# Where a depthwise convolution's taps run: from VectorE, ScalarE and GpSimd to diagonal products on TensorE, inside a mixed decoder block

## The chip, the cores and the metric

One core of a Trainium2 chip runs the whole block for 1024 tokens. The metric is the device time of one execution in microseconds; lower is better. The kernel before takes 3563.5 us (median of three runs, 3561.2 to 3568.37).

## What is computed

One decoder block over x (1024 tokens, 1024 channels), in float32:

```python
u = modulate(rmsnorm(x, norm_mix_g), sh_mix, sc_mix)
p = u @ w_in
y_conv = conformer_conv(p[..., :1024], ...)   # GLU, causal depthwise conv of 31 taps, LayerNorm, SiLU; 512 channels
y_rwkv = rwkv7_mix(p[..., 1024:], ...)        # linear recurrence over tokens, 8 heads of 64
x = x + gt_mix * (concat([y_conv, y_rwkv]) @ w_out)
u = modulate(rmsnorm(x, norm_ffn_g), sh_ffn, sc_ffn)
x = x + gt_ffn * peer_ffn(u, ...)             # product keys choose 8 x 16 of 16384 experts per token
return rmsnorm(x, final_g)
```

The change concerns one line of it, the depthwise convolution: each of 512 channels is filtered with its own 31 weights, `y[t, ch] = sum_j w[j, ch] * in[t - 30 + j, ch] + b[ch]`. Channels lie on partitions, so that 512 channels are four blocks of 128 partitions, and a tap is a multiply-add with one scalar per partition over the tokens of a step.

## The kernel before

All work is written as Python generators ("streams") that yield one instruction at a time. At build time a planner (`Issue.go`, L250) always takes the stream whose next instruction could start first by its own table of durations, and hands the instruction to a scheduler that orders each engine's queue by priority among what is ready. `AHEAD` (L77) moves instructions of some streams forward by a number of places: the recurrence (b), the expert choice (d) and the taps by 300, fetching and using expert rows by 1000; others not at all. At run time each engine works its queue strictly in that order.

The program has two stages.

First stage. Tokens go in five steps (`MACROS`, L65: 128, 128, 256, 256, 256 tokens, that is tiles 0; 1; 2 and 3; 4 and 5; 6 and 7 of 128 tokens).
- Stream a (L549 to L612) multiplies u by w_in (PSUM tile `pA`): first the 14 blocks for the recurrence, written to `xs`, then the 8 blocks of the convolution, whose gated result is `yin` (one buffer, with 30 tokens of the step before in front). It begins `yin` of a step only when the convolution of the step before is over (L602).
- The taps streams (L655 to L689) filter `yin` into `cb`, one 128-channel block after the other. `CONV` (L74) names for each of the four blocks the way it takes: v is VectorE, one multiply-add per tap; g is ScalarE and GpSimd, where ScalarE scales a shifted `yin` into `tap` and GpSimd adds it to `cb`; p is TensorE, below.
- Stream l (L615 to L651) normalises `cb` over channels through PSUM tile `pL` (one buffer) and writes the first half of `ym`.
- Stream b (L698 to L949) runs the recurrence tile by tile, strictly one after the other since each needs the state of the last; many small dependent products (PSUM `pB`) with VectorE and ScalarE steps between them. It writes the second half of `ym` (`ym<-y`).
- Stream c (L952 to L1038) multiplies `ym` by w_out (`pC<-ym,wtC`) when both halves of a step are there, then forms the expert queries (`pC<-uC,wtC`, `pC<-kt,qT`); stream d (L1041) chooses the experts on VectorE and GpSimd.
- For tiles 0, 3, 6 and 7 (`GATHER`) the chosen experts' rows are fetched by GpSimd DMAs (`row`) and used on VectorE (`row<-row,u`, `acc<-row,hj,acc`), in both stages. For tiles 1, 2, 4 and 5 streams g and h turn the choice into a gate matrix through one-hot products (`pA<-onea,oneb`), written to DRAM.

Second stage. Once the first-stage streams a, b, l, y, g, h and the taps are over and all w_out products are done (L1382), tiles 1, 2, 4 and 5 are run through all 16384 experts on TensorE (`ph`, `po`, `pC<-ch`), while the remaining rows are used beside it.

The way p, there already for a block marked p: for each tap ScalarE writes a diagonal matrix, `ident` scaled by the tap's weight (`dg`, 128x128, L660), in pairs that alternate between the buffers of `sqL` and `rsL`; TensorE adds `dg` times the shifted `yin` into one `pL` tile (L663), and after 31 taps ScalarE moves the sum to `cb` with the bias (L664).

Of the kernel before, what the change touches and what calls it, by code (L numbers as in the profile page):

```python
# [70 lines left out]
BIAS = {('use', 'DVE'): 0.0, ('useg', 'POOL'): 0.0, ('a', 'PE'): 0.0}  # L71
DoneDict = dict
ORDER = 'blcdaghy'
ROWS, PSA, CONV = 3, 2, 'vvgg'  # L74
HG = (2, 8)

AHEAD = {('fetch', None): 1000, ('use', None): 1000, ('useg', None): 1000, ('b', None): 300, ('d', None): 300, ('taps', None): 300}  # L77
# [1526 lines left out]
```

## Time and profile before

| | us |
|---|---|
| three runs | 3561.2, 3563.5, 3568.37 |
| profiled execution | 3577.81 |
| its span, first to last instruction | 3576.1 |
| TensorE busy (matmul) | 3119.0 (87%) |
| VectorE busy | 2709.2 (76%) |
| GpSimd busy | 2107.5 (59%) |
| ScalarE busy | 1571.2 (44%) |

In the views PE is TensorE's matmuls, PEld its weight loads, DVE is VectorE, ACT ScalarE, POOL GpSimd. A float32 product is recorded as two MATMUL passes. Nearly every instruction goes through one helper, so that lines say little (L220) and tile names, written out<-in, tell the work. Matmul ends are modelled, so that a busy PE need not be a PE at its peak; PEclk is the granted TensorE clock as a share of 2.4 GHz.

### The profile page before, as it was taken

The page shows a single profiled execution, that of the slowest core. Times are in us where ns is not written, and L with a number is a line of the kernel's source. Part 1 is how long each engine was busy: PE and PEld are TensorE (multiplying, and loading weights), DVE is VectorE, ACT ScalarE, POOL GpSimd, SP SyncE. Part 2 cuts the span into 40 slices and gives each one's busy share as a digit, 9 for nine tenths or more (in the row PEclk, how much of TensorE's full clock was granted, in tenths as well). Part 3 has the DMA queues.
Part 4 walks back from the last instruction along what each step waited for, and adds up shares of the span by engine and source line. Part 5 has one row for each costly group of instructions (what it writes and reads, how often), then busy time and mean ns, then how long its engine had stood idle before and what let it go on. Part 6 is the DMA issues. An engine that isn't in the chain of part 4 may idle for free. (4 is left out here: it accounts for less than half of the span.)

```text
span 3576.1 us, 54020 instructions
## 1 busy us (share of the span) xinstructions
PE 3119.0 (87%) x18460; PEld 2553.7 (71%) x18460; DVE 2709.2 (76%) x5824; ACT 1571.2 (44%) x3831; POOL 2107.5 (59%) x2024
## 2 busy tenths in 40 slices
PE   4999998896899989786783799999999999999996
PEld 4788776775787767665672577777777777777784
DVE  5755888899868878888899977676666777776664
ACT  3445636537554534643764333333333333333332
POOL 0304647579754745667776866565655665665561
PEclk9798988896899988877896899999999999999998
DMA  6654776774677436656787699898988989999982
GB/s 200 218 184 153 282 261 216 272 273 176 213 267 271 145 107 221 239 202 212 277 311 267 220 327 327 314 319 297 324 310 311 331 312 312 336 324 315 324 275 83
DMA packets 423938, 923.02 MB, mean 258 GB/s; under 512 B 30448, under 2 KB 263024, under 8 KB 354032
## 3 DMA queue, kind: packets, MB, share of 16 engines
q0 software_dynamic: 73728, 536.90, 41.0%
q1 hardware_dynamic: 349936, 382.67, 33.2%
q8 instruction: 147, 2.41, 0.3%
q14 instruction: 127, 1.04, 0.1%
HBM read 873.33 MB, written 46.14 MB: 257 GB/s over the span
## 5 line engine op out<-in xcount | busy, mean ns | idle before, releaser
L220 POOL DMA_INDIRECT row<-in_peer_uv_dram,idx x512 | 542.9, 1060 | 464.8 <-DVE ap L220 165.2
L220 POOL TENSOR_TENSOR vl<-v,vh 128x512 fp32r<-128x512 f32 x256 | 329.3, 1292 | 217.3 <-ACT vh L220 211.9
L220 POOL TENSOR_TENSOR wl<-w,wh 128x1024 fp32r<-128x1024 f32 x128 | 307.7, 2404 | 184.2 <-ACT wh L220 183.9
L220 DVE SCALAR_TENSOR_TENSOR ap<-row,hj,ap 128x1024 f32<-128x1024 f32 x280 | 360.0, 1286 | 65.4 <-ACT hj L220 64.2
L220 DVE CUSTOM_DVE_ANT_0 row<-row,up 128x1024 f32<-128x1024 f32 x283 | 344.1, 1216 | 66.3 <-DMA row<-in_peer_uv_dram,idx 65.4
L220 PE MATMUL pA<-uA,wtA 128*128 128x256 f32 (+1 forms) x1760 | 359.8, 358 | 8.8 <-ACT xs L220 5.0
L220 DVE SCALAR_TENSOR_TENSOR acc<-row,hj,acc 128x1024 f32<-128x1024 f32 x224 | 324.0, 1446 | 44.2 <-ACT hj L220 43.3
L220 POOL TENSOR_TENSOR cb<-cb,tap 128x256 f32<-128x256 f32 (+1 forms) x300 | 244.9, 817 | 153.3 <-ACT tap L220 137.0
L220 PEld LDWEIGHTS pA<-uA,wtA 128*128 128x128 f32 x1760 | 297.6, 203 | 48.0 <-ACT xs L220 5.5
L220 PE MATMUL ph<-uh,wh 128*128 128x512 f32 x1024 | 273.2, 412 | 57.1 <-ACT wh L220 50.1
L220 ACT ACTIVATE hj<-hj 128x1 f32<-128x1 f32 x512 | 101.4, 200 | 449.8 <-DVE hj L220 448.8
L220 ACT CAST vh<-v 128x512 fp32r<-128x512 f32 x256 | 155.2, 617 | 308.4 <-DMA v<-in_peer_uv_dram 181.5
L220 PE MATMUL pC<-uC,wtC 128*128 128x256 f32 (+1 forms) x1280 | 276.4, 372 | 16.0 <-ACT s L220 8.9
L220 DVE CUSTOM_DVE_ANT_0 row<-row,u 128x1024 f32<-128x1024 f32 x171 | 242.6, 1421 | 49.0 <-DMA row<-in_peer_uv_dram,idx 48.9
L220 PEld LDWEIGHTS ph<-uh,wh 128*128 128x128 f32 x1024 | 202.8, 200 | 105.6 <-ACT wh L220 50.4
L220 PE MATMUL po<-ch,vh 128*128 128x512 f32 x512 | 210.4, 411 | 66.0 <-ACT ch L220 39.2
L220 PEld LDWEIGHTS pC<-uC,wtC 128*128 128x128 f32 x1280 | 228.1, 213 | 50.1 <-ACT s L220 10.8
L220 PE MATMUL ph<-ul,wh 128*128 128x512 f32 x1024 | 258.2, 389 | 0.0
L220 PE MATMUL ph<-uh,wl 128*128 128x512 f32 x1024 | 257.6, 394 | 0.0
L220 ACT CAST wh<-w 128x1024 fp32r<-128x1024 f32 x128 | 134.1, 1049 | 217.5 <-PE ph L220 131.1
L220 PEld LDWEIGHTS ph<-uh,wl 128*128 128x128 f32 x1024 | 196.6, 192 | 42.2
L220 DVE TENSOR_TENSOR ph<-ph,gt 128x256 f32<-128x256 f32 x256 | 110.0, 430 | 147.9 <-ACT ph L220 146.0
(323 smaller groups left out, 7548.9 us busy)
## 6 DMA issues: line engine op xcount, KB each, us to landing
v<-in_peer_uv_dram SPq DMA_DIRECT2D x256, 256.0 KB, 6.2
w<-in_peer_uT_dram SPq DMA_DIRECT2D x128, 512.0 KB, 5.4
wtA<-in_w_in_dram SPq DMA_DIRECT2D x220, 256.0 KB, 3.9
wtC<-in_w_q_dram SPq DMA_DIRECT2D x160, 256.0 KB, 4.7
Gd<-stg SPq DMA_DIRECT2D x32, 1024.0 KB, 5.7
gt<-Gd SPq DMA_DIRECT2D x31, 1024.0 KB, 13.4
wtC<-in_w_out_dram SPq DMA_DIRECT2D x80, 256.0 KB, 3.2
wtC<-in_ada_w_dram SPq DMA_DIRECT2D x64, 256.0 KB, 3.9
```

The source lines that it names most:

```text
L220: r = op.fn(*op.a, **op.k)
```

## The change

One letter string: every one of the four channel blocks takes the way p.

```diff
-ROWS, PSA, CONV = 3, 2, 'vvgg'
+ROWS, PSA, CONV = 3, 2, 'pppp'
```

`stream_taps` is made once for each letter in `CONV` (L1373), so that two streams (g and v) become one, which does the four blocks one after the other; `taps_dve` and `taps_pool` are no longer called. The function that is now called for all four:

```python
def taps_pe(yin, o, c, n):
    ps = pL()[:, :n]
    for j in range(TAPS):
        if j % 2 == 0:
            dg = tl(act, [128, 2, 128], "dg", tag=("sqL", "rsL")[j // 2 % 2])
        yield A.activation(dg[:, j % 2, :], ident, AF.Copy, scale=cv("dw_w", c * TAPS + j, 1))
        if j % 2 or j == TAPS - 1:
            for q in range(j - j % 2, j + 1):
                yield PE.matmul(ps, dg[:, q % 2, :], yin[:, c, q:q + n], start=q == 0, stop=q == TAPS - 1)
    yield A.activation(o, ps, AF.Identity, bias=cv("dw_b", c, 1))
```

## Rows read from the trace of the kernel before

**Rows 1.** Page parts 1 and 2: busy us and share; PE in 40 slices.

```profile
PE 3119.0 (87%) x18460; PEld 2553.7 (71%) x18460; DVE 2709.2 (76%) x5824; ACT 1571.2 (44%) x3831; POOL 2107.5 (59%) x2024
PE   4999998896899989786783799999999999999996
```

**Rows 2.** Busy time in four stretches: stretch, length, busy us by engine, PEclk, DMA.

```profile
0.00:100.00 100.00, 53.99 (x364) 49.53 (x365) 52.92 (x153) 34.97 (x105) 9.94 (x29) 1.00 0.67 213
100.00:1290.00 1190.00, 1083.42 (x8328) 893.51 (x8328) 943.76 (x2231) 625.53 (x1657) 693.87 (x779) 0.87 0.64 220
1290.00:1968.00 678.00, 505.38 (x3541) 422.25 (x3539) 585.30 (x1807) 353.28 (x816) 451.33 (x489) 0.81 0.68 238
1968.00:3576.00 1608.00, 1476.17 (x6232) 1188.45 (x6232) 1127.25 (x1636) 557.41 (x1255) 952.34 (x728) 0.96 0.86 298
```

**Rows 3.** Timeline of DVE: ends of recurrence tiles 0, 5, 7 (start, us).

```profile
229.81 1.12 DVE L220 SCALAR_TENSOR_TENSOR ym<-y,col,pB 128x128 f32<-128x128 f32 x4
...
1271.62 1.11 DVE L220 SCALAR_TENSOR_TENSOR ym<-y,col,pB 128x128 f32<-128x128 f32 x4
...
1659.12 0.33 DVE L220 SCALAR_TENSOR_TENSOR ym<-y,col,pB 128x128 f32<-128x128 f32 x1
```

**Rows 4.** Timeline of PE: queries, w_out, one-hot products, second stage's start.

```profile
1256.38 0.71 PE L220 MATMUL pC<-kt,qT 128*128 128x128 f32 x4
...
1257.56 2.61 PE L220 MATMUL pC<-ym,wtC 128*128 128x128 f32 x21
...
1703.36 0.61 PE L220 MATMUL pA<-onea,oneb 128*128 128x128 f32 x4
...
1917.63 0.77 PE L220 MATMUL pA<-onea,oneb 128*128 128x128 f32 x2 [2.27 <-DVE onea L220]
1968.46 2.07 PE L220 MATMUL ph<-uh,wh 128*128 128x512 f32 x4 [50.06 <-ACT wh L220]
```

**Rows 5.** Busy time in the stretches of recurrence tiles 3, 5 and 6.

```profile
633.00:872.00 239.00, 201.97 (x1423) 163.09 (x1422) 215.15 (x467) 129.12 (x351) 176.41 (x174) 0.84 0.71 248
...
1080.00:1273.00 193.00, 176.17 (x1289) 141.12 (x1288) 166.81 (x473) 90.77 (x232) 108.18 (x113) 0.89 0.55 193
1273.00:1466.00 193.00, 175.65 (x1367) 142.02 (x1366) 152.92 (x477) 83.25 (x202) 108.85 (x123) 0.86 0.53 185
```

**Rows 6.** Groups by shape: taps on three engines (busy us, mean ns, idle before).

```profile
L220 POOL TENSOR_TENSOR cb<-cb,tap 128x256 f32<-128x256 f32 x180 | 179.0, 995 | 43.5 <-ACT tap L220 35.5 <-ACT hj L220 0.4
...
L220 DVE SCALAR_TENSOR_TENSOR cb<-yin,col,cb 128x256 f32<-128x256 f32 x180 | 124.8, 712 | 0.6
...
L220 ACT ACTIVATE tap<-yin,col 128x256 f32<-128x256 f32 x180 | 89.6, 505 | 72.0 <-POOL cb L220 71.3
...
L220 POOL TENSOR_TENSOR cb<-cb,tap 128x128 f32<-128x128 f32 x120 | 65.9, 549 | 109.8 <-ACT tap L220 101.4 <-ACT pb L220 2.3
...
L220 ACT ACTIVATE tap<-yin,col 128x128 f32<-128x128 f32 x120 | 46.1, 398 | 16.5 <-POOL cb L220 12.5
...
L220 DVE SCALAR_TENSOR_TENSOR cb<-yin,col,cb 128x128 f32<-128x128 f32 x120 | 45.0, 400 | 1.4
```

**Rows 7.** Groups by shape: products and a scaling like those that are added.

```profile
L220 PE MATMUL pA<-uA,wtA 128*128 128x256 f32 x1056 | 262.7, 402 | 5.0 <-ACT xs L220 4.3 <-DVE yin L220 0.5
...
L220 PE MATMUL pA<-uA,wtA 128*128 128x128 f32 x704 | 97.1, 291 | 3.8 <-ACT uA L220 2.1 <-DMA wtA<-in_w_in_dram 1.0 <-ACT xs L220 0.6
...
L220 ACT ACTIVATE kk<-xs,col 128x128 f32<-128x128 f32 x32 | 10.5, 391 | 4.8 <-DVE y L220 4.8
```

**Rows 8.** Busy time and granted clock in three stretches of 100 us.

```profile
100.00:200.00 100.00, 94.47 (x877) 77.34 (x877) 68.33 (x139) 52.21 (x135) 35.21 (x63) 0.74 0.60 194
200.00:300.00 100.00, 99.85 (x883) 87.00 (x882) 58.64 (x152) 45.38 (x127) 11.63 (x19) 0.97 0.57 177
...
800.00:900.00 100.00, 66.45 (x315) 52.30 (x314) 96.17 (x160) 72.07 (x169) 91.54 (x79) 0.71 0.52 183
```

**Rows 9.** Waits between 100 and 1290 us: total, times, longest.

```profile
ACT tap L220 <- POOL cb L220: 83.9, 99, 4.1
```

## The prediction

> **What bounds the kernel now.** I read the page first: PE is the busiest engine, and its slices show two regimes, an uneven stretch up to about slice 22 and then nines to the end [rows 1]. The timeline of PE dates the border: the last one-hot product of the first stage starts at 1917.63 us, and after one gap of 50 us the expert products start at 1968.46 [rows 4]. The stretches say what each part is short of [rows 2]. From 1968 on PE is busy 1476 of 1608 us at a clock of 0.96: nothing of the change lies there, and it starts as late as the first stage ends. So the question is only by how much the first 1968 us get longer or shorter.
>
> Within them the taps run between 100 and 1290 us. There PE is busy 1083 of 1190 us (91%), DVE 944 (79%), POOL 694, ACT 626. After 1290 no tap is left; DVE is the fullest engine (585 of 678, 86%) and PE has 173 us idle.
>
> What passes the delay on are two chains. The recurrence goes tile by tile: tile 0 ends at 231, tile 5 at 1273, tile 7 at 1659 [rows 3], some 200 us each. Stream c is the other: the queries of tiles 2 and 3 end at 1257, and the w_out products of tiles 4 and 5 start in the same microsecond [rows 4], 15 us before tile 5 itself ends (those first instructions are of tile 4). From there queries, expert choice and one-hot products of tiles 4 and 5 follow (one-hots 1703 to 1918), and with them the first stage ends. Both chains meet near 1273 with hardly any slack between them. Stream c has no place ahead of others, so it gets what PE time is left over.
>
> **Part by part.** *Added on PE.* 31 taps x 4 blocks x 5 steps are 620 products; two steps of 128 tokens make 248 with 128 columns, three steps of 256 make 372 with 256. The nearest rows are the w_in products of the same shape and type in the same stretch [rows 7]: 1056 passes are 528 products of 256 columns in 262.7 us, 0.498 us each; 704 passes are 352 of 128 columns in 97.1 us, 0.276 us each. So 372 x 0.498 + 248 x 0.276 = 185 + 68 = 254 us at the clock of that stretch.
>
> *Added on ACT.* 620 scalings of a 128x128 tile at 0.391 us [rows 7] are 242 us, and 20 evictions at about 0.5 us (the nearest row is the 128x256 `tap`, 0.505 [rows 6]) another 10.
>
> *Removed.* DVE loses 124.8 + 45.0 us and ten first taps, some 174 us; POOL loses 179.0 + 65.9 = 245 us; ACT loses 89.6 + 46.1 us and ten first taps, some 141 us [rows 6]. ACT's net is +111 us, 737 of 1190, 62%: it stays far from full. Per block and step the scalings take 31 x 0.39 = 12 us of ACT against 15.4 us (256 columns) or 8.6 us (128) of PE, so that in the wide steps PE sets the pace and in the two narrow ones ACT does.
>
> *Moved waits.* ACT stood 83.9 us in front of `tap` because POOL had not freed its buffer [rows 9]; that goes. In its place ACT waits at `dg` for the pair of products before last, and behind it in ACT's queue stand the recurrence's copies, which PE waits for. No row shows that wait; its bounds are 0 and the 83.9 us that it replaces, and I take it as equal, so no change, since both are a two-deep buffer with an in-order consumer. PE gets a new wait at the head of its queue, for ACT's `dg`; behind it stand the products of a, b and c. Bounded by 0 and by the gap between the two paces in the narrow steps, 8 x (12 - 8.6) = 27 us; I take 0, because other streams' products can be queued between the pairs. `pL` has one buffer and is now used 20 times more; each eviction (0.5 us) delays the taps alone. No DMA is added or removed.
>
> *What lies beside other work.* Between 100 and 1290 PE has 107 us idle. If all of it took taps, 254 - 107 = 147 us of PE work would be too much. Two things shrink that. The clock: it is 0.87 there, 0.97 in a full stretch, 0.71 in one where PE has 34 us idle, but also 0.74 in one that is 94% busy [rows 8], so fullness alone doesn't settle it. I take 0.90, a third of the way to the full stretch: (1083 + 254) x (1 - 0.87/0.90) = 45 us. And work that may go later: the taps of tiles 6 and 7 (124 x 0.498 = 62 us) are needed only with tile 7, near 1659, but they stand 300 places ahead and I let 25 us of them move past 1290, where PE has room; bounds 0 and 62.
>
> *The relief of DVE and POOL.* The recurrence has steps on DVE, and the taps stood among them with the same 300 places. But tiles 6 and 7, without any tap beside them, take 193 and 193 us, and tile 5, with the taps of the last step, 193 as well [rows 3, 5]. So I count the relief at 0; its bound is tile 3, where DVE was busy 215 of 239 us [rows 5], 239 - 193 = 46 us. Expert rows may be used earlier; they aren't what ends either stage, so 0.
>
> **Sum.** 147 - 45 - 25 = +77 us on the first stage, passed whole to the end: the stretch from 1290 to 1968 is DVE's and moves as a block. On the profiled execution's own 3577.8 us (span 3576.1) that is 3655. That execution is 14.3 us above the median of the runs, so for a measured median: 3563.5 + 77 = 3640.
>
> **Rivals.** *1. Faster: TensorE's clock pays for the taps.* If PE, filled with full-width products, holds 2.4 GHz through 100 to 1290, its 1083 us of work take 1083 x 0.87 = 942, and 248 us are free against the 254 x 0.87 = 221 that come. PE then bounds nothing, and what shows is the relief of DVE, 46 us in tile 3: 3563.5 - 46 = about 3518. It decides from a clock of about 0.98. For it: 0.97 between 200 and 300. Against: 0.74 between 100 and 200 with PE 94% busy, which has the small 64x64 products of the recurrence in it, and those stay [rows 8]. [...]
>
> *2. Much slower: the taps' full price.* The idle time stays, because it is waiting for DVE and ACT results in the chains, and the taps, with equal standing, go in front of the recurrence: up to 254 us, 3710 to 3820. For it: c is starved first, and its queries are on the chain. Against: the tap pairs leave ACT one at a time and cannot block PE for long.
>
> *3. No change.* The convolution itself is not waited for late in the stage (its last step ends near 1290 and is used near 1659 [rows 2, 3]), and stream a has slack; if the 254 us fall into that slack and the idle time, the two chains don't notice: 3560 to 3590. Against: PE's 107 us are less than half of what is asked.
>
> **Numbers.** Forecast (+30 to +150): 0.58. Rival 1: 0.17. Rival 2: 0.18. Rival 3: 0.07. The range leaves out the far ends of rivals 1 and 2: 3530 to 3760. A measurement of this kernel can tell about 0.2% (7 us) from no change. Faster by more: rival 1, 0.17. Within: most of rival 3, 0.05. Slower: 0.78.
>
> **What would show it.** In the profile after: 1240 passes into `pL` from `dg`, near 250 us; PE above 95% busy from 100 us to about 1360, with a clock near 0.90; the end of recurrence tile 5 and of the queries of tiles 2 and 3 both later by some 50 to 90 us; the last one-hot product near 1995 and the second stage as long as before, 1608 us. DVE between 100 us and the taps' end near 60 to 65% instead of 79%. I am wrong if the tiles with taps get shorter than 193 us (rival 1), if the first stage ends after 2110 (rival 2), or if the second stage changes its length by more than 15 us, which no step here allows for.

## The result and the profile after

The changed kernel takes 3701.2 us (median of four runs, 3687.1 to 3713.7); the kernel before, run beside it, 3562.4. The ratio is 1.0406, 95% interval 1.0358 to 1.0453: slower by some 139 us (1.0453 and 1.0358 make that 128 to 161). The direction and the range were right. The forecast was 3640, so 61 us of the loss were not in it.

The profiled execution of the changed kernel took 3704.6 us (span 3702.8), that of the kernel before 3577.8 (span 3576.1): 126.7 us to be placed. Page parts 1 and 2 of after, to hold against [rows 1]:

```profile
PE 3257.6 (88%) x19700; PEld 2689.3 (73%) x19700; DVE 2503.4 (68%) x5486; ACT 1657.1 (45%) x4190; POOL 1881.0 (51%) x1736
...
PE   5999999999999999994774079999999999999997
```

Up to the 18th slice the row is nines: what was uneven before is filled. Then come slices of 4 and 7, as there are some of 3 to 8 in the kernel before, and a new thing: a slice with a 0. The stretches show both (columns as in [rows 2]):

```profile
100.00:1290.00 1190.00, 1154.92 (x9132) 968.52 (x9131) 733.56 (x1849) 648.87 (x1837) 423.07 (x472) 0.94 0.63 217
100.00:1638.00 1538.00, 1491.73 (x11660) 1247.55 (x11660) 1018.39 (x2596) 855.75 (x2379) 618.08 (x665) 0.94 0.63 219
...
2009.00:2149.00 140.00, 5.99 (x24) 4.92 (x24) 114.43 (x245) 33.44 (x77) 101.56 (x113) 0.50 0.73 246
```

From 100 to 1290 us PE is busy 1155 of 1190 (97%) at a clock of 0.94, where it was 1083 at 0.87 [rows 2]; VectorE falls from 79% to 62%. The third line is the 0: 140 us in which PE works 6 and VectorE 114. The timeline of PE says what it stood in front of (start, us, names, in brackets the idle time and what ended it), and the waits of PE (total, times, longest) that this is its longest by far:

```profile
2006.34 2.54 PE L220 MATMUL pA<-onea,oneb 128*128 128x128 f32 x8 [1.65 <-DVE best L220]
2139.91 1.11 PE L220 MATMUL pD<-ident,acc 128*128 128x128 f32 x4 [131.03 <-DVE acc L220]
2142.24 1.11 PE L220 MATMUL pD<-ident,acc 128*128 128x128 f32 x4 [1.22 <-DVE x L220]
2144.67 3.76 PE L220 MATMUL pD<-x,onesD 128*128 128x128 f32 x16 [1.31 <-DVE x L220]
2149.21 2.11 PE L220 MATMUL ph<-uh,wh 128*128 128x512 f32 x8 [0.78 <-DVE x L220]
```

```profile
PE pD L220 <- DVE acc L220: 131.0, 1, 131.0
```

The last run of one-hot products starts at 2006 and ends at 2009; the kernel before has its last at 1918 [rows 4]. Behind it stand the eight transposes of `acc`, the finished sum of expert rows of tile 3 (`tile_end`, L1320; the transposes, L1335). Only then come the expert products. VectorE adds that tile's last row at 2138.57. In the kernel before, the transposes of tiles 3, 6 and 7 are among the program's last products, none of them ahead of this one,

```profile
3489.28 0.60 PE L220 MATMUL po<-ident,acc 128*128 128x128 f32 x4
```

and the only thing ahead of the first expert product is the 50 us wait for its weights [rows 4]. So the first expert product moves from 1968 to 2149.

Where the 126.7 us are, from the two timelines of PE: last one-hot product +91 (1918 to 2009, its end), gap ahead of the first expert product +90 (50 to 140), first to last `ph` product -36 (1532 to 1496), what follows it -18 (75 to 57.5). The last two give back part of the second: 256 rows instead of 217 are used when the expert products start, and one tile end less is left for the end.

The first 91, by an account of PE from 100 us to the end of the queries of tiles 4 and 5 (their last `pC<-uC,wtC`), which are at 1544 before and 1638 after, +94. The stretch of before, to hold against the second line above, and the taps of after by shape and the scalings on ACT (busy us, mean ns of one, idle before):

```profile
100.00:1544.00 1444.00, 1302.99 (x9963) 1072.34 (x9962) 1149.99 (x2823) 746.71 (x1945) 850.87 (x935) 0.86 0.63 218
```

```profile
L220 PE MATMUL pL<-yin,dg 128*128 128x256 f32 x744 | 200.5, 409 | 7.4 <-ACT dg L220 5.7 <-ACT cb L220 1.6
L220 PE MATMUL pL<-yin,dg 128*128 128x128 f32 x496 | 83.8, 301 | 0.5 <-ACT dg L220 0.4
...
L220 ACT ACTIVATE dg<-ident,col 128x128 f32<-128x128 f32 x620 | 210.0, 393 | 89.2 <-PE pL L220 85.4 <-DVE ym L220 2.0 <-DVE col L444 0.3
```

The taps add 200.5 + 83.8 = 284 us. The other work shrinks from 1303 to 1492 - 284 = 1207, that is by 95, while the granted clock rises from 0.86 to 0.94. Idle time shrinks from 141 to 46, also by 95. 284 - 95 - 95 = 94 comes out by construction, since a stretch is busy plus idle time; it says where the time went, not why. And the two stretches don't hold the same work: without the taps that of after has 10420 passes, that of before 9963. From the start to the last one-hot product both have the same 12228 passes besides the taps' 1240 (before, then after):

```profile
0.00:1918.40 1918.40, 1642.79 (x12228) 1365.29 (x12228) 1539.00 (x3996) 996.41 (x2544) 1126.76 (x1255) 0.86 0.65 224
```

```profile
0.00:2008.90 2008.90, 1797.65 (x13468) 1507.85 (x13468) 1397.33 (x3768) 1085.80 (x2944) 908.35 (x988) 0.91 0.65 225
```

Over this equal work PE is busy 155 us longer for 284 us of taps, and idle 64 less (276 to 211): +91. By the single records of the two traces, 61 of the 129 us between 284 and 155 are taps whose recorded time lies under that of other products, and 68 are the other products' own time, which falls from 1643 to 1575 at a clock of 0.91 instead of 0.86. Since the ends of matmuls are modelled, this split is rough.

### The profile page after: what moved, and what is told of

It reads as the page before. It is cut to its first block, busy times and chain, and to the rows that moved or that the text cites. A ratio compares the mean times of both kernels' runs of the same rounds, so it can differ in the third digit from the quotient of the medians.

```text
span 3702.8 us, 56003 instructions
## 1 busy us (share of the span) xinstructions
PE 3257.6 (88%) x19700; PEld 2689.3 (73%) x19700; DVE 2503.4 (68%) x5486; ACT 1657.1 (45%) x4190; POOL 1881.0 (51%) x1736
## 5 line engine op out<-in xcount | busy, mean ns | idle before, releaser
L220 DVE SCALAR_TENSOR_TENSOR acc<-row,hj,acc 128x1024 f32<-128x1024 f32 x254 | 345.2, 1359 | 74.0 <-ACT hj L220 72.2
L220 DVE SCALAR_TENSOR_TENSOR ap<-row,hj,ap 128x1024 f32<-128x1024 f32 x252 | 323.7, 1284 | 48.3 <-ACT hj L220 47.4
L220 DVE CUSTOM_DVE_ANT_0 row<-row,up 128x1024 f32<-128x1024 f32 x256 | 310.8, 1214 | 66.9 <-DMA row<-in_peer_uv_dram,idx 66.4
L220 PEld LDWEIGHTS pA<-uA,wtA 128*128 128x128 f32 x1760 | 288.5, 197 | 41.1 <-issue 4.9
L220 DVE CUSTOM_DVE_ANT_0 row<-row,u 128x1024 f32<-128x1024 f32 x192 | 259.8, 1353 | 81.0 <-DMA row<-in_peer_uv_dram,idx 80.9
L220 PE MATMUL pL<-yin,dg 128*128 128x256 f32 (+1 forms) x1240 | 284.3, 365 | 7.9 <-ACT dg L220 6.0
L220 POOL TENSOR_TENSOR xs<-xs,pb 128x128 f32<-128x128 f32 x112 | 65.4, 599 | 407.5 <-ACT xs L220 300.5
L220 PE MATMUL pC<-uC,wtC 128*128 128x256 f32 (+1 forms) x1280 | 260.5, 354 | 11.4 <-ACT s L220 6.7
L220 ACT ACTIVATE dg<-ident,col 128x128 f32<-128x128 f32 x620 | 210.0, 393 | 89.2 <-PE pL L220 85.4
L220 PEld LDWEIGHTS pL<-yin,dg 128*128 128x128 f32 x1240 | 214.5, 205 | 38.3 <-ACT dg L220 9.1
```

The lines of the kernel that those rows point to most:

```text
L220: r = op.fn(*op.a, **op.k)
```

## The experiments

Each kernel was re-planned as a whole by its edit, so besides what the edit is for, other instructions move a little too. Runs of one kernel scatter by some 1% (the kernel before from 3538 to 3573 in one set of seven). Single profiles therefore don't tell shifts of 20 us or less apart; ratios carry their intervals. And a new plan can by itself cost some per cent, as the second kernel and the one with one block show below, so that a single kernel's time is not the price of its edit to the microsecond.

**Is the wait for tile 3 the loss, or do the taps lose it in any case?** First, in the changed kernel, the end of tile 3 was put behind eight expert products.

```diff
-            if not second:                       # stream_fetch
+            if not second and not m:
-  d["H"] >= NE - 28 * (len(left) - 1 - n)         # stream_end
+  d["H"] >= (8 if not n else NE - 28 * (len(left) - 1 - n))
```

> All taps on TensorE; the only edit is that the end of gather tile 3 (its transposes on TensorE) is put into the second stage, behind the first eight expert products, instead of in front of them. My theory (of the 139 us, about 90 are TensorE standing at the head of its queue for the last rows of tile 3): the gap in front of the first expert product goes from 140 us to about 50, some 35 us of it are given back because more rows are left for the second stage, so 3640 us, between 3625 and 3660. Rival (the rows end when they end, and the gap only shows it; the second stage gets longer by as much): 3690 to 3710.

Measured: 3657.2 us, ratio 1.0279 (1.0230 to 1.0328), on the theory's side. The 131 us wait is gone, the gap ahead of the expert products is 43 us, the first of them is at 2067 instead of 2149. Of the 139 us some 44 went (1.0406 less 1.0279, in parts of 3550), less than the 90 of the gap. That is what the account above says: a gap that is filled gives up the rows that were used in it.

**The same edit on the kernel before,** which has no tap on TensorE, so that the wait can be seen by itself.

> The kernel before (taps on VectorE, ScalarE and GpSimd) with the same edit on the end of tile 3, which in the kernel before stood at the very end of the program. My theory: the start of the second stage does not move (no gap was there beyond 50 us), and the end of the program has one tile less to do, 18 us by the tails of the two profiles: 3545 us, 3535 to 3555. Rival (the edit gains something by itself in any order, as much as in the other kernel): 3500 or less; or nothing at all, 3555 to 3570.

Measured: 3636.1 us, ratio 1.0208 (1.0152 to 1.0264). The expectation was missed by 90 us, and the miss shows the mechanism. Waits of PE and stretches of this kernel:

```profile
PE po L220 <- DVE acc L220: 76.4, 1, 76.4
```

```profile
1968.00:2081.00 113.00, 91.64 (x348) 70.97 (x347) 100.64 (x122) 33.76 (x74) 93.96 (x88) 0.89 0.72 241
2081.00:2196.00 115.00, 28.38 (x110) 22.02 (x111) 87.92 (x121) 27.10 (x79) 39.72 (x38) 0.64 0.90 321
2196.00:2300.00 104.00, 101.60 (x430) 81.75 (x429) 75.53 (x110) 36.94 (x85) 62.26 (x47) 0.98 0.91 320
```

The first stage is as long as before (last one-hot product 1917, first expert product 1968). Then the transposes of tile 3 come up in PE's queue before its rows are used, and PE stands 76 us, busy 28 of 115. From first to last expert product it takes 1614 us instead of 1532. A kernel without any tap on TensorE becomes 2% slower through the place of eight transposes alone.

**Do the taps cost because they stand ahead of others?** The taps lose their 300 places.

```diff
-AHEAD = {..., ('b', None): 300, ('d', None): 300, ('taps', None): 300}
+AHEAD = {..., ('b', None): 300, ('d', None): 300}
-CONV = 'vvgg'
+CONV = 'pppp'
```

> All taps on TensorE, but the taps no longer stand 300 places ahead. My theory (the late taps of tiles 6 and 7 took TensorE from the queries of tiles 4 and 5): these queries end some 60 to 90 us sooner than in the changed kernel, and so does the last one-hot product; the gap for the rows of tile 3 stays and may grow by part of it: 3640 us, 3610 to 3680. Rival (the added TensorE work counts wherever it stands): last one-hot product within 15 us of the changed kernel, 3690 to 3715.

Measured: 3743.6 us, ratio 1.0527 (1.0483 to 1.0570). The theory falls, and the rival's number is missed too, by 29 us. The queries of tiles 4 and 5 end at 1642 (1638 with the places), the last one-hot product is at 2032, and PE waits 158 us for tile 3's rows:

```profile
PE pD L220 <- DVE acc L220: 158.3, 1, 158.3
```

The queries gain nothing when the taps lose their places; the larger wait makes the time longer.

**Both edits.**

> All taps on TensorE, taps not ahead, and the end of tile 3 in the second stage: both edits. My theory: the sum of the two, 3580 to 3610, that is still 20 to 50 us above the kernel before, the remainder being TensorE's own load. Rival (TensorE's added work of 254 to 284 us is the whole cause): not below 3660.

Measured: 3696.3 us, ratio 1.0416 (1.0362 to 1.0471), 86 us above what was expected, on the rival's side. First expert product at 2055, but PE then waits 26 us for tile 3's rows, and is busy 27 of the 58 us from 2174 to 2232. Eight expert products are too few here as well.

**The end of tile 3 behind forty expert products,** where its rows must have been used.

```diff
-  d["H"] >= (8 if not n else ...)
+  d["H"] >= (40 if not n else ...)
```

> All taps on TensorE; the end of gather tile 3 stands behind 40 expert products in the second stage, some 470 us after its start, where its rows are surely done. My theory (two costs: 91 us of TensorE load in the first stage, and TensorE standing for tile 3's rows wherever its end stands too early, 131 us in the changed kernel, 31 us in the run with its end behind eight products): no wait for the rows is left on TensorE, first expert product near 2060, 3615 to 3640 us. Rival (the rows' work is what the second stage is short of, so that the wait only moves on): 3650 to 3700.

Measured: 3667.9 us, ratio 1.0338 (1.0294 to 1.0383): on the rival's side. (The 31 us of the expectation are not in the trace of the first kernel, whose PE doesn't stand for these rows at all; 26 us are in that of the fourth.) No wait for tile 3's sum is left on PE, and the first expert product follows the last one-hot product (1996) after 43 us of waiting for weights:

```profile
2039.07 6.53 PE L220 MATMUL ph<-uh,wh 128*128 128x512 f32 x16 [43.08 <-ACT wh L220]
```

So with the wait out of the way the first expert product is still 71 us later than before (2039 to 1968), and the loss is still 3.4%, some 120 us. In the profiled execution, 93 us longer than that of the kernel before, 71 lie ahead of that product and 22 behind it (1630 instead of 1608). Most of these 22 are lost early: in the 461 us after that product PE is idle 60 us, against 42 in the kernel before; why is open.

**The end where the kernel before has it,** as the last products of the program (the first half of the first edit alone).

> The changed kernel, with the end of tile 3 among the last instructions of the program, where the kernel before has it. Theory: only the taps' price is left, the first stage 70 to 90 us longer and the second as long as before: about 3630 (3615 to 3645). Rival: the expert stage of the changed kernel is longer for another reason (it was 20 us longer with that end behind 40 expert products), and the time is 3650 to 3680.

Measured: 4012.4 us, ratio 1.1282 (1.1223 to 1.1340). Neither side expected this, and it doesn't count for the taps. Its first stage bears the fifth kernel out (last one-hot product 2006, first expert product 2050). But then the sum of tile 3 keeps its buffer until the program's end. The rows of the last tile, fetched from 2832 to 3464 us in the kernel before, are fetched up to 4000 here, nearly all of them after the last `ph` product (3549), and PE waits for their sum:

```profile
PE po L220 <- DVE acc L220: 414.1, 1, 414.1
```

In the two kernels sums go into buffers by the stage in which the planner builds their last row (L1308): in the kernel before the sum of tile 3 got the second stage's buffer, here the one that tile 6 needs. The trace agrees: no row is added from 2831.5 on, and the next, the last of tile 6, comes right behind the last transposes of tile 3:

```profile
3551.07 0.49 PE L220 MATMUL pC<-ident,acc 128*128 128x128 f32 x3
```

```profile
3551.94 1.27 DVE L220 SCALAR_TENSOR_TENSOR acc<-row,hj,ap 128x1024 f32<-128x1024 f32 x1
```

It was not tried by itself.

**Taps at half the passes.** `yin` and `dg` are made fp32r, so that a product is one pass and not two (620 passes, in the changed kernel 1240). (That this rounds the taps' operands was assumed; no run here measured it.) In this kernel the end of tile 3 stands at the program's end by itself.

```diff
-  yin = YIN[t0] = tl(act, [128, 4, 256 + TAPS - 1], "yin")
+  yin = YIN[t0] = tl(act, [128, 4, 256 + TAPS - 1], "yin", dt=F32R)
-  dg = tl(act, [128, 2, 128], "dg", tag=...)
+  dg = tl(act, [128, 2, 128], "dg", tag=..., dt=F32R)
```

> All taps on TensorE, but with the diagonals and the convolution's input rounded to fp32r, so that each of the 620 products is one pass instead of two slower ones; the output is thereby rounded differently. Number of instructions for ScalarE and all orders of waiting are kept; tile 3's end falls at the end of the program here, as in the kernel before. My theory (TensorE's time is the whole cost in the first stage): tap products 70 to 130 us instead of 284, last one-hot product between 1870 and 1930 instead of 2009, 3510 to 3570 us. Rival (the diagonal writes on ScalarE and the waits for them are the cost, or the place of the taps in the queues): last one-hot product after 1970, 3620 or more.

Measured: 3600.5 us, ratio 1.0132 (1.0100 to 1.0164), between the two. The number of ScalarE's scalings is that of the changed kernel; the taps' time on PE is not:

```profile
L220 PE MATMUL pL<-yin,dg 128*128 128x256 f32 (+1 forms) x620 | 156.7, 351 | 15.0 <-ACT dg L220 13.1 <-ACT cb L220 1.7
```

In the kernel before, a pass of 512 fp32r columns takes 389 ns (`ph<-uh,wh`, median of 1024) and one of 512 float32 columns 592 (`pB<-ysq,oneh`, median of 16). The taps' passes are not shorter in that proportion: 351 ns here against 365 in the changed kernel, means over both widths.

157 us of taps move the first expert product to 2003, +35. Against the fifth kernel, at as many scalings, the first expert product comes 36 us earlier and the ratio falls from 1.0338 to 1.0132: a good part of the price goes with the passes on TensorE. That all of it does isn't shown. Tile 7 of the recurrence ends at 1654 here and at 1659 in the kernel before, so the 35 us are lost behind it, from there to the last one-hot product. In that stretch VectorE is the fullest engine in both, and has 35 us more to do here (columns as in [rows 2], the kernel before first):

```profile
1659.40:1918.40 259.00, 198.81 (x1099) 173.12 (x1097) 231.85 (x692) 161.42 (x375) 188.88 (x184) 0.87 0.76 269
```

```profile
1653.90:1960.70 306.80, 214.74 (x1101) 184.43 (x1099) 266.51 (x759) 171.25 (x410) 220.12 (x237) 0.78 0.72 259
```

**Two blocks of four,** once in place of GpSimd's (`CONV = 'vvpp'`) and once in place of VectorE's (`CONV = 'ppgg'`).

> Half of the change: the two blocks of ScalarE and GpSimd go to TensorE, VectorE keeps its two. My theory (142 us of TensorE work, of which idle time and the higher clock take most, half of 95 + 95 at least): last one-hot product 0 to 50 us later than before, no gap because tile 3's end stays at the end of the program, 3560 to 3610 us. Rival (relief of VectorE is what pays, GpSimd's is worth nothing): at least 25 us above the run in which VectorE's blocks go.

> The other half: VectorE's two blocks go to TensorE, ScalarE and GpSimd keep theirs. My theory (relief of either engine is worth little, TensorE's load counts): within 20 us of the run with the other half, 3560 to 3610 us. Rival (VectorE stood on the recurrence's path with 74 of some 1270 us in the kernel before): below 3550.

Measured: 3576.4 us, ratio 1.0062 (1.0036 to 1.0088), and 3595.8 us, ratio 1.0135 (1.0092 to 1.0177). Both lie in the range of their theories, and both rivals fall. 142 us of taps on PE in both, first expert product +24 and +16 in the profiled executions. The difference between the two ratios (0.0 to 1.4%, by the ends of the intervals) goes the other way than that between the two profiles; the first profiled execution is the longest of its nine (3603), the second the shortest of its four (3577). So which engine is relieved is not settled by them.

**One block of four** (`CONV = 'vvgp'`).

> One of the four blocks on TensorE (310 passes, about 70 us), taken from GpSimd; VectorE keeps two. Theory: the price grows faster than the load, because the first block finds idle time and a higher clock: 3545 to 3565. If the price were in proportion to the load, it would be a quarter of 139 us: 3580 to 3590. If GpSimd's relief counted, below 3540.

Measured: 3635.3 us, ratio 1.0240 (1.0182 to 1.0298). The expectation was missed by 70 us: half the load of the two kernels above costs twice to four times as much. Its queries of tiles 4 and 5 end at 1539, earlier than before, tile 7 at 1667, 8 later, and the time is lost behind tile 7 (last one-hot product 1962). There VectorE has 30 us more to do than in the kernel before, and is again the fullest engine:

```profile
1667.20:1962.20 295.00, 212.81 (x1098) 184.51 (x1097) 261.47 (x805) 160.54 (x366) 237.03 (x246) 0.81 0.72 257
```

Why more is left for it there is open. The taps' time on PE, 73 us, can't be the cause of it all, since 142 us of taps cost 22 to 48 us in the two kernels above.

**TensorE's load alone.** The taps stay where the kernel before has them, and 1240 passes of the same shape, with `ident` as weights, are done beside them and thrown away.

```diff
+    def taps_extra(yin, n):
+        ps = pL()[:, :n]
+        for j in range(TAPS):
+            yield PE.matmul(ps, ident, yin[:, 0, j:j + n], start=j == 0, stop=j == TAPS - 1)
...
+                if kind == "x":
+                    yield from taps_extra(CB[t0][0], n)
+                    done["taps"] += n // 128
...
-        yield Wait(lambda: done["taps"] == 4 * (t0 // 128) + 4 * nt)
+        yield Wait(lambda: done["taps"] == 8 * (t0 // 128) + 8 * nt)
```

> The kernel before, with its taps where they are, and beside them the same number of products of the same shape on TensorE (1240 passes into pL), with the identity as weights and thrown away; ScalarE scales no diagonal tile. All ends of gather tiles stand where they stand in the kernel before. Theory: TensorE's time is the price, and what VectorE, ScalarE and GpSimd are spared is worth nothing, so the last one-hot product comes 70 to 95 us later than in the kernel before, the gap ahead of the expert products stays near 50 us, and the median is about 3635 (3615 to 3655). Rival: the price lies in ScalarE's 620 scalings and PE's wait for them; then products that wait for nothing fill PE's idle time, and the median stays below 3590.

Measured: 3708.1 us, ratio 1.0428 (1.0371 to 1.0486). The rival falls: products that wait for nothing cost as much as the whole change. But the theory's number was missed too, by 73 us. Taps and first expert product of this kernel:

```profile
L220 PE MATMUL pL<-yin,ident 128*128 128x256 f32 (+1 forms) x1240 | 251.4, 353 | 0.0
```

```profile
2121.25 4.13 PE L220 MATMUL ph<-uh,wh 128*128 128x512 f32 x9 [36.57 <-ACT wh L220]
```

251 us on PE move the queries of tiles 4 and 5 to 1676 (+132) and the first expert product by 153. The changed kernel, without its wait for tile 3, has +71. The other engines' relief in the changed kernel may be part of the difference. Another part is that a step of the convolution here waits for both kinds of taps, so that its last is over at 1833 instead of 1627; this kernel doesn't part the two.

**The relief alone.** One tap of 31 is left on VectorE and on GpSimd, the other thirty are left out on every engine.

```diff
-        for j in range(1, TAPS):          # taps_pool and taps_dve
+        for j in range(0):
```

> The kernel before with one tap of 31 on VectorE and GpSimd; the other thirty are left out, on every engine. Theory: the taps of before are hidden beside a recurrence that is bound elsewhere, so taking them away saves at most the 46 us by which the fullest tile is longer than a tile without taps: 3500 to 3550. Rival: the taps of before cost the first stage as much as TensorE's do, and the time falls below 3480.

Measured: 3501.1 us, ratio 0.9846 (0.9784 to 0.9908), some 55 us below the kernel before (33 to 77 by the interval), at the lower end of the theory's range. The first expert product moves by the same 55, from 1968 to 1913:

```profile
1913.09 5.76 PE L220 MATMUL ph<-uh,wh 128*128 128x512 f32 x16 [47.33 <-ACT wh L220]
```

So the taps of the kernel before are not free. ScalarE's 300 scalings of `yin` are left out too, which the change replaces by 620 others; this kernel is thus not the change's relief alone. What the taps cost shows in the tiles of the recurrence. Ends of tiles 5 and 7 here (last instruction of each):

```profile
1190.49 0.85 DVE L220 SCALAR_TENSOR_TENSOR ym<-y,col,pB 128x128 f32<-128x128 f32 x3
...
1604.10 0.59 DVE L220 SCALAR_TENSOR_TENSOR ym<-y,col,pB 128x128 f32<-128x128 f32 x2
```

Tiles 1 to 5 take 962 us from the end of tile 0 (229) to 1191, against 1042 in the kernel before (231 to 1273): tile 5 ends 81 earlier. Tiles 6 and 7 give 27 of that back, tile 7 ends 55 earlier, and so does the first expert product.

The runs together, from the profiled executions (us; "queries end" is the last `pC<-uC,wtC`, "first expert product" against 1968):

| kernel | taps on PE | queries of 4, 5 end | last one-hot | first expert product | ratio |
|---|---|---|---|---|---|
| no taps at all | 0 | 1436 | 1865 | -55 | 0.985 |
| before | 0 | 1544 | 1918 | 0 | 1 |
| one block | 73 | 1539 | 1962 | +34 | 1.024 |
| two for VectorE's | 142 | 1560 | 1936 | +16 | 1.014 |
| two for GpSimd's | 143 | 1577 | 1946 | +24 | 1.006 |
| four, fp32r | 157 | 1560 | 1960 | +35 | 1.013 |
| four, end of tile 3 behind 40 | 279 | 1622 | 1996 | +71 | 1.034 |
| after | 284 | 1638 | 2008 | +181 | 1.041 |
| before, and four on PE | 251 | 1676 | 2078 | +153 | 1.043 |

## Why the prediction was right in sign and short by 61 us

*The taps on PE, 254 us.* 284 measured. The rows taken for the price [rows 7] were of the right shape, but gave 0.498 and 0.276 us a product; the taps took 200.5 / 372 = 0.539 and 83.8 / 248 = 0.338, and at a higher clock (0.94 instead of 0.87). Short by 30. The same 1240 passes with `ident` as weights, which wait for nothing, took 251.

*ACT.* 242 us of scalings predicted at 391 ns each; they took 393 ns each, and since their records overlap, 210 us of busy time. ACT never became the bound (649 of 1190 us). The wait at `dg`, taken as equal to the 83.9 us that it replaces [rows 9], measured 85.4. Right, though no row had shown it.

*Idle time.* All 107 us between 100 and 1290 were to be used; 72 were (1190 - 1155 = 35 are left), 95 up to the end of the queries of tiles 4 and 5, and 64 over the whole first stage.

*Clock, 45 us.* 0.90 was taken, 0.94 came, and the first stage's other 12228 passes took 68 us less in all. That is the evidence that the first rival had on its side, and still not enough for it: it needed 0.98. With full-width tap products in it, tile 2's stretch, 382 to 642, runs at 0.95:

```profile
382.00:642.00 260.00, 252.04 (x1893) 214.28 (x1892) 161.03 (x452) 149.68 (x436) 109.50 (x152) 0.95 0.72 247
```

How busy PE is goes with the clock only in part: it is 0.50 in the 140 us in which PE of the changed kernel works 6, but 0.74 and 0.97 in two stretches of the kernel before that are 94% and nearly 100% busy [rows 8]. The first rival's time, 3518, was not seen. The views give the clock as a share alone; the prediction's 2.4 GHz fits them as an estimate: in the kernel before, with 0.50 granted (2633 to 2638 us), fp32r expert products of 512 columns start 0.427 us apart, 1.2 columns per ns, which would be 2.4 at full speed. With 1.00 granted (2502 to 2505 us) they start 0.227 us apart, 2.26 per ns.

That the taps' products are what raised the clock is not shown. In the same stretch, 100 to 1290, it is 0.95 and 0.93 with two blocks on PE and 0.89 with four in fp32r, but also 0.91 in the kernel without any taps:

```profile
100.00:1290.00 1190.00, 1114.76 (x8989) 917.95 (x8989) 795.81 (x2043) 536.62 (x1411) 506.87 (x550) 0.91 0.67 230
```

*25 us moved past 1290, where PE has room.* The step of the sum that failed outright. The whole last step went there, not 25 us of it, because its `yin` came at 1300 to 1405 instead of 1123 to 1188; and there was no room: from 1290 to 1638 PE is as full as ahead of it.

```profile
1290.00:1638.00 348.00, 336.81 (x2530) 279.03 (x2530) 284.83 (x748) 206.88 (x544) 195.01 (x194) 0.94 0.64 225
```

Of the 173 us idle after 1290 [rows 2], 138 lie behind 1544, the end of the queries of tiles 4 and 5, too late for the taps. The third kernel says the same: without their 300 places the taps were not cheaper, the time was longer.

*Relief of DVE and POOL, 0 with a bound of 46.* The kernel without taps puts it at some 55; its interval, 33 to 77, doesn't say whether the bound held, but 0 is excluded (ScalarE's share is in it). The reasoning compared one tile with taps, tile 5, with tiles 6 and 7, and its own rows say more: tiles 1 to 5 took 1273 - 231 = 1042 us [rows 3], 208 each against 193, so that five tiles with taps were 77 us longer than five without. Leaving the taps out shortened them by 80 (1042 to 962), and tile 7 and the first expert product came 55 earlier. The queries of tiles 4 and 5 came 108 earlier (1544 to 1436), of which half was not passed on.

*What was to pass the delay on.* "Tile 5 and the queries of tiles 2 and 3 later by 50 to 90": tile 5 ended at 1300, 27 later than before, and the queries of tiles 2 and 3 (their last `pC<-kt,qT`) at 1274, 17 later. The delay came up one step further on, in the queries of tiles 4 and 5 (+94) and in tile 7 (1718, +59). The last one-hot product, expected near 1995, was at 2008. One sign of rival 1 came without it: tile 1 took 157 us, less than 193; tiles 2, 4, 5 and 6 took 220 to 260.

*The sum for the first stage, +77.* Over equal work the account gives 284 - 129 - 64 = 91 at the last one-hot product. At the first expert product, with the end of tile 3 out of the way, it is +71 (fifth kernel) and +82 (the one with the ends last). So the size was nearly right, but as a sum of errors, which is luck: the taps too cheap by 30, the gift of the clock and of overlapping products too small by 84 (45 for 129), that of idle time too large by 43 (107 for 64), and a gift of 25 that did not exist. By the kernels at both ends it is made of other terms: from no taps at all to all taps on PE is +126 to +137, and of that the kernel before already pays 55.

*The second stage unchanged.* Wrong, and by the criterion that the prediction had set itself (15 us): it begins 90 us later after the last one-hot product and is 54 shorter from there on, so that 36 of the 126.7 come from it. If the first expert product is the first stage's end, as with 1968 in the prediction, its bound of 2110 for rival 2 was passed too (2149). The prediction took the order of PE's queue at the border as given. The order is planned anew for every kernel, and the change moved eight transposes that need the last expert row from the end of the program to the front of the stage. The change costs some 24 us less with them elsewhere (1.0406 less 1.0338, intervals of 0.5% to either side each; some 44 less in the first kernel), and a like move, behind eight expert products, costs the kernel before 2%.

*The rivals.* "Much slower" (3710 to 3820) was close, and for another reason than given: not the idle time stayed, but a wait was added. "No change" needs a slack that is not there: with 157 us on PE the kernel is already 1.3% slower.

*What stays open.* Why VectorE has more left to do behind tile 7 with one block on PE, which costs more than two blocks do, and with fp32r taps; how the price goes with the load below four blocks; and the 22 us that the second stage is longer in the fifth kernel. The prediction's 0.2% for what a measurement can tell was too fine as well: the kernel before scatters by 1%. With the wait gone and half the passes the change is still a loss, and no kernel here with a full convolution was faster than the kernel before.

## What to carry to other kernels

Of the busy engine's 173 us of idle time after 1290, 138 came too late for the added work: count the idle time ahead of the point at which the chain needs the result, not in the whole stage. Where a planner orders the queues, a change in one stage can move an instruction with a late input to the front of another, as it moved eight transposes here, with a wait of 131 us: look at what stands first in the full engine's queue at each border, and whose data it needs. And to price taking work off an engine, add up all the steps that have it, not one of them: one tile showed 0 us where five together showed 77; and leave the work out in an experiment, which gave 55.

## What was not expected of the hardware

With 284 us of full-width tap products added, the granted clock of the stretch from 100 to 1290 us was 0.94 instead of 0.87, and the first stage's other 12228 passes took 68 us less; but a kernel with no taps at all, and so with another plan, ran the stretch at 0.91. And fp32r operands made of a tap one pass instead of two of nearly the same length each (620 passes of 351 ns, 157 us, against 1240 of 365 ns, 284 us).
